# A hybrid decoder step on one Trainium2 core: another order for the 28 units of the input projection

## The chip, the cores and the metric

The kernel runs on one core of one Trainium2 chip. The metric is device time in microseconds. Three runs of the kernel before took 1135.55 to 1137.87 us, median 1137.05 us.

## The reference, cut to what matters

One layer of a decoder trunk over 512 prompt tokens and 32 sample tokens (8 sequences of 4), model width 1024, all float32:

```
x <- LN1(alpha*x + 0.5*SwiGLU_1(x))
x <- LN2(alpha*x + W_out[concat(attn_group(x), hgrn_group(x))])
x <- LN3(alpha*x + 0.5*SwiGLU_2(x))
z = x @ W_in;  columns of z: [q_att | k_att | v_att | q_hg | f_hg | i_hg | g_hg], 512 each
attn_group: 8 heads of 64, rotary q and k, dilated windows (128,1), (512,4), (2048,16),
            combined by their softmax denominators; sample tokens also read a key/value cache
hgrn_group: 4 heads of 128, f = lb + (1-lb)*sigmoid(f_hg), S_t = diag(f) S_{t-1} + (1-f) outer i_hg,
            o_t = S_t^T silu(q_hg); then per-head RMSNorm, times hg_norm_g * silu(g_hg)
```

The rotated keys and the values, the new caches and the HGRN states are outputs too.

## The kernel before, in words

Everything is kept transposed: features on the 128 partitions, the 544 tokens (16 sample, 512 prompt, 16 sample) along the free dimension, in two halves `a` of 272. A matmul of two float32 operands is done as three: each operand is split into a high part (ScalarE copies it to the rounded type, L332) and a low part (VectorE subtracts, L334), and `chunk` issues high*high, high*low and low*high (L315 to L317).

The stages are the first FFN, the mix stage (`mix`), the output projection (`project`) and the second FFN. The mix stage is built around the input projection, whose 3584 columns are cut into 28 units of 128 columns. One unit is one transfer of 512 KB (`ws`), one split, and for each half 8 chunks of 3 matmuls into a PSUM bank `ps_d` (there are two of these), which is then evacuated. A ring holds the split weights of four units (`R = 4`). The tuple `WIN` gives the order of the units. An entry is `(c, i)`: `c` is a group of 128 columns (two attention heads, or one HGRN head), called chunk here, and `i` is 0 query, 1 key, 2 value of attention, 3 forget gate, 4 query, 5 value (input), 6 output gate of HGRN. What hangs on a unit is emitted as soon as its second half is done (function `mixed` in `mix`):

- 0 and 1: evacuation to `raw` (two buffers for all queries, keys and values), rotation (`rope`: four small DMAs that swap partitions, a POOL and two VectorE operations), then stacks for the score matmuls (`q_done`, `k_done`). The low part of the keys, `klo`, has one buffer.
- 2: the values are transposed into `vn` (one buffer, `v_done`), then prompt attention of the chunk is emitted (`att_prompt`): eight steps (four query blocks, two heads) of score matmuls (L702), a masked maximum (L706), an exponential (L708), normalisation (L710), transposes (L679), a copy (L717), and value matmuls per block (L726). After chunks 1 and 3 the sample attention of two chunks follows (`att_sample`): score matmuls against the key cache (L754), value matmuls against the value cache (L784, L790).
- 5: the HGRN head is emitted (`hgrn`). Its work tiles have one buffer; the product of decays `E1` (the trace calls it E) is written by a scan at the start (L822) and last read by the state update at the end (`update`, L976).
- 6: the gate. If the unit after a value unit `(c, 5)` is `(c, 6)`, the head's end is emitted with the gate ahead of the norm; else the norm and the state update are emitted at once and the gate is multiplied in when its unit arrives:

```
if a == 1:
    part["end"] = self.hgrn(c, part)
    if WIN[j + 1] != (c, 6):
        part["end"] = part["end"]()
...
if a == 1 and i == 6:
    o[4 + c] = part["end"](part["gs"])
```

The multiplication of the gate is L964, the norm's factor is put on by L813. The results are `o[0..3]` (attention) and `o[4..7]` (HGRN).

`project` splits `o` in the order `KORD = (0, 4, 1, 5, 2, 6, 3, 7)` and contracts over these eight chunks in the same order, so a unit of the output projection can start with `o[0]` and needs `o[3]` and `o[7]` last.

The order on each engine is not the order of the program: a scheduler that plays the program through a timeline of its own while the kernel is built picks, on each engine, the earliest emitted instruction that is ready in that timeline, and hands out buffers in the same way. On the chip each engine then follows the list so made. Where a unit stands in `WIN` sets the priority of all that hangs on it.

Of the kernel before, what the change touches and what calls it, by code (L numbers as in the profile page):

```python
# [64 lines left out]
def free(t, offset, dims):  # L65
# [3 lines left out]


WIN = (
    (0, 0), (0, 4), (0, 3), (0, 5), (0, 6), (0, 1), (1, 3), (0, 2), (1, 4), (1, 0), (1, 1), (1, 5), (1, 2), (2, 3),
    (2, 0), (2, 4), (2, 1), (2, 2), (1, 6), (2, 5), (2, 6), (3, 0), (3, 1), (3, 2), (3, 4), (3, 3), (3, 5), (3, 6),
)


# [1139 lines left out]
```

## Time and profile before

| what | value |
|---|---|
| median of three runs | 1137.05 us (1135.55 to 1137.87) |
| the profiled execution | 1141.93 us, span 1140.1 us |
| mean granted TensorE clock | 0.982 |
| busy: TensorE, weight loads, VectorE, ScalarE, POOL | 96, 92, 68, 50, 33% of the span |
| mix stage: first and last evacuation of an input-projection unit | 400.3 and 655.5 us |
| first normalisation matmul of the output projection | 703.8 us |

Rows of the timeline read: start in us, duration in us, engine, line, operation, output <- inputs, shape, count, and in brackets how long the engine was idle before it and what ended that. Rows of stretches read: window, then for PE, PEld (weight loads), DVE (VectorE), ACT (ScalarE) and POOL the busy us and instruction count, then the granted clock of TensorE, the share of the DMA engines and GB/s.

### The profile page before, as it was taken

To read this page: it belongs to the slowest core of one execution; us is meant where nothing else is said; L and a number is where in the kernel's file an instruction comes from. 1 tells how busy PE (TensorE), PEld (TensorE's weight loads), DVE (VectorE), ACT (ScalarE), POOL (GpSimd) and SP (SyncE) were. 2 spreads that over 40 slices of the span, in tenths; PEclk is the share of its full clock that TensorE was granted. 3 is DMA by queue.
4 is the path that set the end of the run, shared out by engine and by line. 5 is a ranking of instruction groups with operands and counts; after the bars stand their busy time and mean duration, and the time that the engine had idled before them with its cause. 6 is when DMAs were issued, how large, how long until landed. Compare 5 with 4: busy or idle time off the path is not lost.

```text
span 1140.1 us, 21927 instructions
## 1 busy us (share of the span) xinstructions
PE 1094.2 (96%) x8666; PEld 1047.1 (92%) x8666; DVE 780.7 (68%) x1282; ACT 570.6 (50%) x1123; POOL 373.8 (33%) x420
## 2 busy tenths in 40 slices
PE   7899999999999999999999988988999999999995
PEld 7899999999999988878997858978999999999995
DVE  6868857865776965664746646788687578567766
ACT  5435533552554675566456643465355235425544
POOL 2513412430343444231411301345143125214336
PEclk9899999999999999999999978999999999999998
DMA  7344444454415385376736624504533432332122
GB/s 247 104 130 154 154 144 148 126 194 149 128 44 195 112 276 168 122 261 228 238 105 223 240 98 161 184 17 171 171 130 102 136 111 89 89 103 92 41 72 79
DMA packets 46168, 163.49 MB, mean 143 GB/s; under 512 B 6512, under 2 KB 10224, under 8 KB 45040
## 3 DMA queue, kind: packets, MB, share of 16 engines
q1 hardware_dynamic: 46064, 162.08, 43.0%
q8 instruction: 68, 1.11, 0.4%
q14 instruction: 36, 0.29, 0.1%
HBM read 150.79 MB, written 42.60 MB: 170 GB/s over the span
## 4 chain that ended last, share of the span: by engine, by line
PE 82%; DVE 7%; DMA 4%; ACT 3%; issue 2%; POOL 2%; SPq 0%; POOLq 0%; DVEq 0%; ACTq 0%
PE ps_d L278 20%; PE ps_h L278 10%; PE ps_d L316 7%; PE ps_d L315 7%; PE ps_d L317 7%; PE ps_a L278 5%; PE ps_a L316 3%; PE ps_a L315 3%; PE ps_a L317 3%; PE ps_h L317 2%; PE ps_h L315 2%; PE ps_h L316 2%; DVE wL L334 2%; PE ps_s L754 1%; PE ps_a L679 1%
## 5 line engine op out<-in xcount | busy, mean ns | idle before, releaser
L334 DVE TENSOR_TENSOR wL<-ws,wH 128x1024 fp32r<-128x1024 f32 (+3 forms) x141 | 174.2, 1236 | 80.8 <-ACT wH L332 77.7
L332 ACT ACTIVATE wH<-ws 128x1024 fp32r<-128x1024 f32 (+3 forms) x141 | 129.3, 918 | 183.4 <-PE ps_d L278 49.3
L1008 POOL TENSOR_TENSOR h<-hx,h 128x272 fp32r<-128x272 f32 x88 | 98.6, 1122 | 159.7 <-ACT h L1007 153.4
L334 DVE TENSOR_TENSOR wL<-sw,wH 128x1024 fp32r<-128x1024 f32 x78 | 117.1, 1503 | 40.2 <-ACT wH L332 40.1
L315 PE MATMUL ps_d<-xH,wH 128*128 128x272 f32 x456 | 136.2, 299 | 4.7 <-ACT xH L332 4.3
L316 PE MATMUL ps_d<-xL,wH 128*128 128x272 f32 x456 | 137.4, 301 | 3.2 <-DVE xL L405 3.0
L317 PE MATMUL ps_d<-xH,wL 128*128 128x272 f32 x456 | 135.2, 297 | 0.5 <-DVE wL L334 0.5
L332 ACT ACTIVATE wH<-sw 128x1024 fp32r<-128x1024 f32 x78 | 82.6, 1059 | 81.8 <-PE ps_d L278 29.5
L225 POOL TENSOR_TENSOR sw<-ws,sw 128x512 f32<-128x512 f32 x38 | 55.3, 1456 | 157.3 <-DVE sw L222 137.5
L315 PEld LDWEIGHTS ps_d<-xH,wH 128*128 128x128 f32 x456 | 87.4, 192 | 9.2 <-ACT xH L332 5.0
L278 PE MATMUL ps_d<-xH,wL 128*128 128x272 f32 x320 | 92.9, 290 | 1.9 <-DVE wL L334 1.9
L316 PEld LDWEIGHTS ps_d<-xL,wH 128*128 128x128 f32 x456 | 87.6, 192 | 7.5 <-DVE xL L405 3.7
L278 PE MATMUL ps_d<-tH,wH 128*128 128x272 f32 x320 | 92.9, 290 | 0.0
L278 PE MATMUL ps_d<-tH,wL 128*128 128x272 f32 x320 | 92.9, 290 | 0.0
L278 PE MATMUL ps_d<-tL,wH 128*128 128x272 f32 x320 | 92.9, 290 | 0.0
L220 POOL TENSOR_TENSOR sw<-ws 128x512 f32<-128x512 f32 x38 | 53.2, 1401 | 120.7 <-issue 48.1
L278 PE MATMUL ps_d<-xL,wH 128*128 128x272 f32 x320 | 92.4, 289 | 0.0
L278 PE MATMUL ps_d<-xH,wH 128*128 128x272 f32 x320 | 92.2, 288 | 0.0
L317 PEld LDWEIGHTS ps_d<-xH,wL 128*128 128x128 f32 x456 | 87.6, 192 | 4.1 <-issue 2.7
L315 PE MATMUL ps_d<-h,wH 128*128 128x272 f32 x240 | 69.2, 288 | 0.0
L317 PE MATMUL ps_d<-h,wL 128*128 128x272 f32 x240 | 69.0, 288 | 0.0
L316 PE MATMUL ps_d<-h,wH 128*128 128x272 f32 x240 | 68.9, 287 | 0.0
(412 smaller groups left out, 3600.8 us busy)
## 6 DMA issues: line engine op xcount, KB each, us to landing
ws<-in_w2gu SPq DMA_DIRECT2D x42, 512.0 KB, 3.9
ws<-in_w1gu SPq DMA_DIRECT2D x41, 512.0 KB, 4.5
ws<-in_win SPq DMA_DIRECT2D x28, 512.0 KB, 4.2
out_ck_out<-in_ck SPq DMA_DIRECT2D x16, 640.0 KB, 5.7
out_cv_out<-in_cv SPq DMA_DIRECT2D x16, 640.0 KB, 5.5
kv<-in_ck SPq DMA_DIRECT2D x16, 640.0 KB, 6.3
kv<-in_cv SPq DMA_DIRECT2D x16, 640.0 KB, 5.0
ws<-in_w1d SPq DMA_DIRECT2D x24, 384.0 KB, 3.2
```

The source lines that it names most:

```text
L220: g.tensor_tensor(s2[:, lo], a21, a22, op=OP.add)
L225: g.tensor_tensor(s2[:, hi], a12, s1[:, hi], op=OP.subtract)
L278: nc.tensor.matmul(ps, w[:, k, :], y, start=first and i == 0, stop=last and i == 2, skip_group_check=True)
L315: mm(o, H[:, k, :], x[0], start=first, stop=False)
L316: mm(o, H[:, k, :], x[1], start=False, stop=False)
L317: mm(o, L[:, k, :], x[0], start=False, stop=last)
L332: a = self.nc.scalar.activation(H, x, AF.Copy)
L334: v = self.nc.vector.tensor_tensor(L, x, H.bitcast(F32), op=OP.subtract)
L679: self.nc.tensor.transpose(out, x, self.ident[:n, :n])
L754: last = mm(ps[w, :384], self.qsz[:, i, s, 32 * (b + x):32 * (b + x) + 32], kc[x][:, i, 2 * s:2 * s + 3].rearrange("p s d -> p (s d)"), st ...
L1008: nc.gpsimd.tensor_tensor(L, x, H.bitcast(F32), op=OP.subtract)
```

## The change

Only the order of the units changes, from the 14th entry on. The first 13 stay. Counted from 0, chunk 1's gate (1, 6) goes from place 18 to 25 and chunk 2's gate (2, 6) from 20 to 26; chunk 3's queries, keys and values go from 21, 22, 23 to 18, 19, 21; chunk 2's HGRN value (2, 5) goes from 19 to 20; chunk 3's HGRN query, forget gate and value go from 24, 25, 26 to 22, 23, 24; chunk 2's attention query and key go from 14 and 16 to 13 and 14, its forget gate and HGRN query from 13 and 15 to 15 and 16. Since (2, 5) and (3, 5) are no longer followed by their own gates, the ends of heads 2 and 3 are emitted without the gate, which is multiplied in afterwards.

```
 WIN = (
-    (0, 0), (0, 4), (0, 3), (0, 5), (0, 6), (0, 1), (1, 3), (0, 2), (1, 4), (1, 0), (1, 1), (1, 5), (1, 2), (2, 3),
-    (2, 0), (2, 4), (2, 1), (2, 2), (1, 6), (2, 5), (2, 6), (3, 0), (3, 1), (3, 2), (3, 4), (3, 3), (3, 5), (3, 6),
+    (0, 0), (0, 4), (0, 3), (0, 5), (0, 6), (0, 1), (1, 3), (0, 2), (1, 4), (1, 0), (1, 1), (1, 5), (1, 2), (2, 0),
+    (2, 1), (2, 3), (2, 4), (2, 2), (3, 0), (3, 1), (2, 5), (3, 2), (3, 4), (3, 3), (3, 5), (1, 6), (2, 6), (3, 6),
 )
```

## The prediction, before the run

> **What bounds the kernel now.** I read the page's engine and clock rows first, then a table of stretches, then the timelines of TensorE, ScalarE, VectorE and the DMA queue through the mix stage.
>
> ```profile
> PE 1094.2 (96%) x8666; PEld 1047.1 (92%) x8666; DVE 780.7 (68%) x1282; ACT 570.6 (50%) x1123; POOL 373.8 (33%) x420
> ...
> 100.00:200.00 100.00, 100.00 (x799) 100.00 (x798) 69.03 (x92) 43.62 (x74) 30.45 (x24) 1.00 0.46 148
> ...
> 660.00:670.00 10.00, 8.34 (x64) 5.43 (x62) 3.20 (x10) 3.23 (x9) 0.00 (x0) 0.80 0.58 188
> 670.00:680.00 10.00, 9.27 (x50) 6.52 (x50) 3.88 (x14) 4.59 (x20) 0.00 (x0) 0.52 0.00 0
> 680.00:690.00 10.00, 3.88 (x29) 2.78 (x27) 6.84 (x19) 5.98 (x14) 0.00 (x0) 0.82 0.00 0
> 690.00:700.00 10.00, 10.00 (x74) 9.53 (x73) 4.82 (x14) 2.70 (x9) 0.00 (x0) 0.83 0.45 141
> ```
>
> TensorE carries the kernel: in a dense stretch it starts 799 matmuls in 100 us, 0.125 us each, so one unit of the input projection (48 matmuls) is 6.0 us. The last rows show the one hole near the change: from 660 to 690 us weight loads fall to 2.8 to 6.5 of 10 us and the granted clock to 0.52. The projection is used up there. What remains runs in two chains, and both have to end before the output projection gets its last two input chunks.
>
> ```profile
> 457.92 0.28 PE L702 MATMUL ps_a<-kst,qst 128*128 128x256 f32 x1
> 515.73 1.09 PE L726 MATMUL ps_o<-aw,vn 128*64 128x128 f32 x16
> 520.71 0.28 PE L702 MATMUL ps_a<-kst,qst 128*128 128x256 f32 x1
> 576.18 1.09 PE L726 MATMUL ps_o<-aw,vn 128*64 128x128 f32 x16
> 580.90 0.28 PE L702 MATMUL ps_a<-kst,qst 128*128 128x256 f32 x1
> 641.46 1.09 PE L726 MATMUL ps_o<-aw,vn 128*64 128x128 f32 x16
> 645.96 0.28 PE L702 MATMUL ps_a<-kst,qst 128*128 128x256 f32 x1
> 694.14 1.09 PE L726 MATMUL ps_o<-aw,vn 128*64 128x128 f32 x16
> ...
> 696.91 0.79 DVE L334 TENSOR_TENSOR xL<-z,xH 128x272 fp32r<-128x272 f32 x2 [0.94 <-ACT xH L332]
> ```
>
> These are the first score matmul and the last value matmul of prompt attention for chunks 0 to 3. Each chunk starts 3.4 to 3.9 us after the one before has ended, because klo and vn have one buffer. From 458 to 695 us attention is one unbroken chain of 57.8, 55.5, 60.6 and 48.2 us (first row to second of each pair), and the output projection's chunk 3 is ready at 697.7 us.
>
> **The change part by part.** Slots are places in the order, counted from 0.
>
> ```profile
> 556.93 0.38 ACT L524 ACTIVATE raw<-ps_d 128x272 f32<-128x272 f32 x1
> 557.71 0.40 ACT L550 ACTIVATE gs<-ps_d 128x272 f32<-128x272 f32 x1
> 563.01 0.38 ACT L550 ACTIVATE gs<-ps_d 128x272 f32<-128x272 f32 x1
> ...
> 570.81 0.37 ACT L539 ACTIVATE iT<-ps_d 128x272 f32<-128x272 f32 x1
> ...
> 581.44 0.38 ACT L550 ACTIVATE gs<-ps_d 128x272 f32<-128x272 f32 x1
> ...
> 598.51 0.38 ACT L524 ACTIVATE raw<-ps_d 128x272 f32<-128x272 f32 x1
> ...
> 611.33 0.38 ACT L524 ACTIVATE raw<-ps_d 128x272 f32<-128x272 f32 x1
> ```
>
> (a) No unit is added or removed: 28 times 6.0 us, 28 weight transfers, the same evacuations, ropes and splits. Sum 0. It is a move, and the rows give the clock time of each slot (slot 17 ends at 556.9, slot 18 at 563.0, 19 at 570.8, 20 at 581.4, 22 at 598.5, 23 at 611.3).
>
> (b) Chunk 2's values stay at slot 17 (556.9), 20 us ahead of the end of attention 1 that gates them; chunk 3's values move from slot 23 to 21 but attention 3 waits for attention 2 (642.5), not for them. So neither attention chain starts earlier: 0.
>
> (c) Chunk 3's queries and keys move from slots 21 and 22 to 18 and 19, three slots (27.7 us by 598.5 less 570.8, some 20 once the 6.8 us of waiting below are taken off). With them go eight rope DMAs, a K output, and the rope and stack work on POOL, VectorE and ScalarE. Sample attention of the second head pair needs exactly these keys:
>
> ```profile
> 605.72 1.50 PE L754 MATMUL ps_s<-kv,qsz 128*32 128x384 f32 x16
> ...
> 663.74 0.35 DVE L710 TENSOR_SCALAR aw<-aw,stat 128x256 f32<-128x256 f32 x1
> 665.20 1.20 PE L784 MATMUL ps_s<-kv,pz 128*32 128x256 f32 x16 [1.54 <-DMA kv<-in_cv]
> 668.01 0.61 PE L679 MATMUL ps_h<-mats,smp 128*32 128x128 f32 x2
> 668.79 0.69 PE L679 MATMUL ps_a<-mats,aw 128*128 128x128 f32 x2
> ```
>
> Its scores begin at 605.7 now and can begin some 20 us earlier; its last value matmuls then lie near 645, under the projection, not at 665. Now they wait for a cache transfer with TensorE empty for 1.54 us, and attention 3's transposes, whose input was ready at 664.09, stand behind them until 668.79: 4.7 us. That wait ends. Bounds: nothing gained (dense matmuls stand there instead) and 4.7. The step it sits in took 7.45 us (661.68 to 669.13); the three before it, with TensorE full, took 15.72, or 5.24 each. I take the difference, -2.2.
>
> ```profile
> 661.68 0.36 PE L702 MATMUL ps_a<-kst,qst 128*128 128x256 f32 x1
> ...
> 669.13 0.67 PE L702 MATMUL ps_a<-kst,qst 128*128 128x384 f32 x1
> ...
> 675.36 0.42 DVE L710 TENSOR_SCALAR aw<-aw,stat 128x384 f32<-128x384 f32 x1
> 675.73 0.82 PE L315 MATMUL ps_d<-xH,wH 128*128 128x272 f32 x2
> 679.04 0.80 PE L679 MATMUL ps_a<-mats,aw 128*128 128x128 f32 x3
> 681.45 1.28 ACT L435 ACT_TABLE_LOAD   x1
> 683.50 0.72 ACT L708 ACTIVATE aw<-aw,stat 128x512 f32<-128x512 f32 x1
> ```
>
> (d) Gates 1 and 2 go from slots 18 and 20 to 25 and 26: 12.0 us of dense work into the tail. On the chain it costs nothing as long as it fills the hole of (660, 690); if it stands in front of attention's own matmuls it costs up to 12. It keeps TensorE busy, so the rows above at a clock of 0.52 run faster: the output-projection matmuls ahead of the transposes hold them from 675.78 to 679.04 (3.3 us); at full clock that is 3.3 x 0.52 = 1.7, so I take -1.5 (bounds 0 and -3.3). Four evacuations (0.8 us ScalarE each) and their VectorE steps also move there; both engines are under 7 of 10 us busy, and if one lands ahead of an exponential it costs 0.8. I take +0.5 (bounds 0 and 3.2). The table load ahead of the exponential at 683.50 stays: 0 (bounds -2.0 and 0).
>
> (e) Queues. The rope DMAs go ahead of later weight transfers on SP's queue and wait there for raw. The weight ring holds four units, 24 us of dense work, which covers that; with the cover gone the longest such wait is 7.1 us:
>
> ```profile
> SPq L627 <- ACT raw L524: 10.0, 3, 7.1
> ```
>
> Sum: -2.2 - 1.5 + 0.5 = -3.2 us. The profiled execution took 1141.93 us, 4.9 above the median of the runs, so it would be 1138.7, and the median 1137.05 would be 1133.9. The terms' ends give -10.0 to +3.2; the 12 us of (d) standing in front of attention are a rival below.
>
> **The rivals.** First, slower: the HGRN chain. HGRN 3 cannot write E until HGRN 2's state update has read it.
>
> ```profile
> 569.14 0.69 DVE L676 TENSOR_TENSOR klo<-raw,kst 64x512 fp32r<-64x512 f32 x1
> ...
> 630.03 1.12 DVE L976 SCALAR_TENSOR_TENSOR st<-st,E,ps_h 128x128 f32<-128x128 f32 x4
> 637.62 1.29 DVE L822 TENSOR_TENSOR_SCAN E<-mats,sf 128x544 f32<-128x544 f32 x1
> ...
> 679.97 0.73 DVE L964 SCALAR_TENSOR_TENSOR z<-z,gs 128x544 f32<-128x544 f32 x1 [4.19 <-ACT z L945]
> ...
> 690.32 0.43 DVE L334 TENSOR_TENSOR xL<-z,xH 128x272 fp32r<-128x272 f32 x1
> ```
>
> HGRN 2's values move from slot 19 to 20, from 570.8 to 581.4. Its update ends 60.3 us after them, so at 641.8. There is a second delay: slot 18 now needs a raw buffer, and of the two one holds chunk 2's values and the other its keys until 569.83. The first half, ready at 557.7, is stuck for 12.1 us; TensorE fills the other ps_d bank by 563 and then has none for up to 6.8 us, so HGRN 2 may end at 648.6. HGRN 3's scan follows (I allow 1 us) at 642.8 to 649.6, where it was 637.62. From scan to split input took 53.1 us; with the gate now after the norm (0.73, the L964 row) chunk 7 is ready at 696.7 to 703.5. It is needed at 699.2 (697.7, and 12 matmuls of chunk 3 ahead of it). So this chain decides from an end of HGRN 2 at 644.3 on, and at its late end it costs 4.3: 1141.4 us. Against it: its transposes at 668.01 stood behind the same cache wait and matmuls, 668.01 less 665.20 plus 1.54, 4.35 us that it gets back if (c) holds; then it decides only from 648.7 on.
>
> On that stuck evacuation the Trainium skill ("PSUM — Partial Sum Buffer", section "Engine vs sequencer instructions") says that ScalarE's queue is strictly first-in first-out, which speaks against the change: attention's exponentials queued behind it would wait too. By that rule the sum would be worse by up to those 12.1 us, if the order put them there; no run here shows it at this place, and the other sentences go without it.
>
> Second, no change: the dense work of the gates stands where the sample matmuls stood, and attention 3 keeps its 48.2 us. For it speaks (b): nothing makes the chain start earlier. 1137 us.
>
> Third, slower by filling: with TensorE full attention 3 takes the mean of chunks 0 to 2, 58.0 us: +9.8, 1146.9. Against it: the total work is the same, and only 12 us are moved.
>
> Fourth, a larger gain through the clock. Busy time from 660 to 700 times what the clock lacked is 8.34 x 0.20 + 9.27 x 0.48 + 3.88 x 0.18 + 10.0 x 0.17 = 8.5 us. If the fillers hold the clock at 1.00 and all of it lies on the chain, 1128.5 us. The Trainium skill ("TensorE: Matmul & The Clock Gate", section "What's actually happening") says that the array falls to half clock after an idle window of about 3.4 us and recovers after one of activity; the 0.52 agrees. Against it: the long holes of 3 us wait on VectorE, and remain.
>
> **How the numbers follow.** The forecast (gain of 2.4 to 7 us, own range 1130.0 to 1134.7) has 0.35 and the clock case 0.10: faster 0.45. No change has 0.27. The HGRN chain has 0.22 and filling 0.06: slower 0.28. Within 0.2% (2.3 us) is what a measurement here cannot tell from no change. Leaving out the outer parts of the clock and filling cases, the range is 1126 to 1145.
>
> **What would show it.** Right: sample attention's last value matmuls (L784) before 655; the clock above 0.8 between 660 and 690; the last L726 some 3 us earlier than 694.1. Wrong: HGRN 3's scan (L822) after 646 and chunk 7's split after chunk 3's; an L524 evacuation waiting near 560 to 570 with TensorE idle; or attention 3 taking more than 50 us.

## The result: 0.9% slower

The changed kernel takes 1146.38 us (median of four runs, 1146.26 to 1149.76) against 1136.30 us: a ratio of 1.0091, 95% interval [1.0071, 1.0111]. Forecast were 1133.9 us and a range of 1126 to 1145; the time lies above both. The profiled execution of the changed kernel took 1149.76 us (span 1147.9), 3.4 above its median, that of the kernel before 1141.93, 5.6 above the new median. From the first normalisation copy behind the mix stage (line L351) to the end of the span both need the same time (1147.9 - 711.3 = 436.6 and 1140.1 - 702.5 = 437.6 us). The first evacuation of an input-projection unit, at 400.5 and 400.3 us, is not late either. So the whole loss arises in the mix stage. What is late in the profile of the changed kernel is so by up to 3.4 us more than in its median run. Because the first profile of before lies high, a second one is set beside it below (before2, 1135.71 us, span 1133.8).

The engines' row of the page after: TensorE starts as many matmuls as before and is busy 3.9 us longer; the other engines do the same work, but for one ScalarE instruction fewer.

```profile
PE 1098.1 (96%) x8666; PEld 1050.6 (92%) x8666; DVE 779.2 (68%) x1282; ACT 567.9 (49%) x1122; POOL 374.0 (33%) x420
```

Stretches of 10 us of the changed kernel, columns as before the prediction (window; PE, PEld, DVE, ACT and POOL busy; granted clock; DMA share; GB/s):

```profile
520.00:530.00 10.00, 7.75 (x67) 6.38 (x65) 5.40 (x14) 7.06 (x19) 3.60 (x12) 1.00 0.18 40
...
570.00:580.00 10.00, 8.01 (x44) 7.58 (x44) 3.49 (x7) 3.44 (x8) 2.94 (x6) 0.66 0.24 76
...
680.00:690.00 10.00, 7.53 (x61) 5.03 (x60) 4.60 (x15) 6.45 (x21) 0.00 (x0) 0.86 0.45 146
690.00:700.00 10.00, 9.03 (x61) 8.08 (x59) 1.38 (x4) 5.00 (x14) 0.00 (x0) 0.80 0.01 2
700.00:710.00 10.00, 7.29 (x33) 6.38 (x32) 7.69 (x21) 0.75 (x2) 0.00 (x0) 0.71 0.33 107
```

The reader is to see two new holes in the middle of the projection (67 and 44 matmuls, where the kernel before starts 96 and 97 by its second profile) and that the tail's hole is not filled but has moved from 660 to 690 to 680 to 710. The timeline of the changed kernel shows what the holes wait for and what becomes late (bracket: idle time ahead of the instruction and what ended it):

```profile
523.99 0.40 PE L315 MATMUL ps_d<-xH,wH 128*128 128x272 f32 x1 [2.25 <-ACT raw L524]
560.43 0.38 ACT L524 ACTIVATE raw<-ps_d 128x272 f32<-128x272 f32 x1
569.48 0.63 PE L679 MATMUL ps_a<-mats,aw 128*128 128x128 f32 x4 [1.86 <-DVE aw L710]
571.34 0.69 DVE L676 TENSOR_TENSOR klo<-raw,kst 64x512 fp32r<-64x512 f32 x1
572.11 0.69 ACT L524 ACTIVATE raw<-ps_d 128x272 f32<-128x272 f32 x2
572.56 0.59 PE L315 MATMUL ps_d<-xH,wH 128*128 128x272 f32 x1 [1.99 <-ACT raw L524]
581.44 1.09 PE L726 MATMUL ps_o<-aw,vn 128*64 128x128 f32 x16
585.30 0.40 ACT L524 ACTIVATE raw<-ps_d 128x272 f32<-128x272 f32 x1
592.51 0.38 ACT L539 ACTIVATE iT<-ps_d 128x272 f32<-128x272 f32 x1
642.73 0.28 PE L702 MATMUL ps_a<-kst,qst 128*128 128x256 f32 x1
653.25 0.34 SPq L978 DMA_DIRECT2D out_ss<-st  x1
654.84 1.28 DVE L822 TENSOR_TENSOR_SCAN E<-mats,sf 128x544 f32<-128x544 f32 x1
660.90 1.07 PE L784 MATMUL ps_s<-kv,pz 128*32 128x256 f32 x16
694.85 1.09 PE L726 MATMUL ps_o<-aw,vn 128*64 128x128 f32 x16
703.20 0.71 DVE L964 SCALAR_TENSOR_TENSOR z<-z,gs 128x544 f32<-128x544 f32 x1
705.51 0.78 DVE L334 TENSOR_TENSOR xL<-z,xH 128x272 fp32r<-128x272 f32 x2
707.62 0.34 SPq L978 DMA_DIRECT2D out_ss<-st  x1
711.32 0.43 ACT L351 ACTIVATE zr<-z 128x272 fp32r<-128x272 f32 x1 [6.62 <-DMA out_ss<-st]
```

Both TensorE holes wait for an evacuation into `raw`. Chunk 3's queries (both halves at 572.11) needed a `raw` buffer, which came free when `klo` of chunk 2 had been made (571.34, ends 572.03). Head 2's values, at 570.8 before, come at 592.51; the write of its state (653.25) and head 3's scan (654.84, before 637.6) are late in turn. Head 3 then ends the stage: its gate (behind the norm now) at 703.20, chunk 7's split at 705.51, state write issued at 707.62, and only when that write has landed does the first copy of the next stage start, 711.32. Attention 3 began 3 us earlier than before and took 52 us. The same events in the second profile of the kernel before:

```profile
570.47 0.37 ACT L539 ACTIVATE iT<-ps_d 128x272 f32<-128x272 f32 x1
575.84 1.09 PE L726 MATMUL ps_o<-aw,vn 128*64 128x128 f32 x16
637.27 1.29 DVE L822 TENSOR_TENSOR_SCAN E<-mats,sf 128x544 f32<-128x544 f32 x1
645.61 0.28 PE L702 MATMUL ps_a<-kst,qst 128*128 128x256 f32 x1
685.27 0.43 DVE L334 TENSOR_TENSOR xL<-z,xH 128x272 fp32r<-128x272 f32 x1
689.72 1.09 PE L726 MATMUL ps_o<-aw,vn 128*64 128x128 f32 x16
692.49 0.79 DVE L334 TENSOR_TENSOR xL<-z,xH 128x272 fp32r<-128x272 f32 x2 [0.94 <-ACT xH L332]
694.71 0.34 SPq L978 DMA_DIRECT2D out_ss<-st  x1
697.83 0.43 ACT L351 ACTIVATE zr<-z 128x272 fp32r<-128x272 f32 x1 [5.05 <-issue]
```

Here chunk 7's split ends at 685.7, ahead of attention's end and of chunk 3's split (692.49). In the changed kernel chunk 3's split starts at 699.48 and chunk 7's, last of all, at 705.51.

### The profile page after: what moved, and what is told of

Its sections match the earlier page's. It is cut to its first block, busy times and chain, and to the rows that moved or that the text cites. A ratio compares the mean times of both kernels' runs of the same rounds, so it can differ in the third digit from the quotient of the medians.

```text
span 1147.9 us, 21933 instructions
## 1 busy us (share of the span) xinstructions
PE 1098.1 (96%) x8666; PEld 1050.6 (92%) x8666; DVE 779.2 (68%) x1282; ACT 567.9 (49%) x1122; POOL 374.0 (33%) x420
## 4 chain that ended last, share of the span: by engine, by line
PE 79%; DVE 9%; ACT 4%; DMA 3%; issue 3%; POOL 1%; SPq 0%; POOLq 0%; DVEq 0%; ACTq 0%
PE ps_d L278 19%; PE ps_h L278 10%; PE ps_d L315 7%; PE ps_d L316 7%; PE ps_d L317 7%; PE ps_a L278 5%; PE ps_a L316 3%; PE ps_a L315 3%; PE ps_a L317 3%; PE ps_h L315 2%; PE ps_h L317 2%; PE ps_h L316 2%; DVE wL L334 2%; PE ps_s L754 1%; PE ps_a L679 1%
## 5 line engine op out<-in xcount | busy, mean ns | idle before, releaser
L332 ACT ACTIVATE wH<-ws 128x1024 fp32r<-128x1024 f32 (+3 forms) x141 | 129.3, 918 | 184.0 <-PE ps_d L278 47.3
L315 PE MATMUL ps_d<-xH,wH 128*128 128x272 f32 x456 | 139.5, 306 | 10.4 <-ACT xH L332 5.9
L317 PE MATMUL ps_d<-xH,wL 128*128 128x272 f32 x456 | 136.9, 301 | 0.5 <-DVE wL L334 0.5
L332 ACT ACTIVATE wH<-sw 128x1024 fp32r<-128x1024 f32 x78 | 82.6, 1059 | 82.5 <-PE ps_d L278 29.3
L225 POOL TENSOR_TENSOR sw<-ws,sw 128x512 f32<-128x512 f32 x38 | 55.3, 1455 | 156.6 <-DVE sw L222 118.1
L315 PEld LDWEIGHTS ps_d<-xH,wH 128*128 128x128 f32 x456 | 89.5, 196 | 16.6 <-ACT xH L332 6.9
L278 PE MATMUL ps_d<-xH,wH 128*128 128x272 f32 x320 | 92.2, 288 | 0.0
L317 PEld LDWEIGHTS ps_d<-xH,wL 128*128 128x128 f32 x456 | 89.5, 196 | 2.4 <-issue 1.2
L315 PE MATMUL ps_d<-h,wH 128*128 128x272 f32 x240 | 69.3, 289 | 0.0
L317 PE MATMUL ps_d<-h,wL 128*128 128x272 f32 x240 | 69.2, 288 | 0.0
```

The source lines that it names most:

```text
L225: g.tensor_tensor(s2[:, hi], a12, s1[:, hi], op=OP.subtract)
L278: nc.tensor.matmul(ps, w[:, k, :], y, start=first and i == 0, stop=last and i == 2, skip_group_check=True)
L315: mm(o, H[:, k, :], x[0], start=first, stop=False)
L317: mm(o, L[:, k, :], x[0], start=False, stop=last)
L332: a = self.nc.scalar.activation(H, x, AF.Copy)
```

## The experiments

Four explanations stood against each other. **The chain (U):** head 2's late values make head 3 late, and head 3 ends the stage. **The end:** only the last piece counts (chunk 7's split, the state update), and could be cut there. **Stalls (R):** TensorE's idle and slow time in the middle is the loss itself, wherever the chains stand. **Filling (F):** the gates moved into the tail stand in front of attention 3. Ratios are to the kernel before on the same chip. The expectations use more letters: H is the chain with chunk 7 as its end, T the end with head 3's state write as its last piece, A attention 3 as the end.

### Is it the end of head 3?

a_no7 gives the output projection chunk 6 where it needs chunk 7. a_no7_noupd also leaves out head 3's state update. a_upd and b_upd emit that update ahead of head 3's norm, in the changed kernel and in the one before.

```
a_no7:        self.split(..., o[min(k, 6)][:, a, :])
a_no7_noupd:  the same, and  if h < 3: update()   (head 3's state is written as loaded)
a_upd, b_upd: if h == 3: update()   # ahead of the norm, instead of after it
```

> Leaves out one wait: the output projection reads chunk 6 again in place of chunk 7 (HGRN head 3), all else of the changed kernel stays. Theory H (HGRN head 3 ends last, its split was 6 us behind that of attention chunk 3, 706.3 against 700.3): 6 us less than the changed kernel, 1139 to 1142. Theory R (the loss is TensorE time lost while evacuations wait for a raw buffer near 522 and 570): unchanged, 1145 to 1148. Theory F (the gate units moved to the end stand in front of attention 3): unchanged, 1145 to 1148.

> The changed kernel; the output projection reads chunk 6 in place of chunk 7, and the state update of HGRN head 3 is left out (its state goes out as it came, right after its load). So neither result of head 3 is waited for at the end. Theory T: the stage ends with attention 3, whose split is near 700: 1136 to 1140. Theory R (the loss is TensorE time lost while evacuations wait for raw): 1144 to 1147. Theory F (gate units stand in front of attention 3): 1144 to 1147.

> The changed kernel with the state update of HGRN head 3 emitted ahead of its norm and not held behind it. Theory T: its write lands before 700, what is left of head 3 is chunk 7 (split near 706), so 3 us less: 1142 to 1144.5. Theories R and F: unchanged, 1145 to 1148.

> The same edit in the kernel before. Theory T: there too the state write landed last (702.4, against 699.5 for the first output-projection unit), so 2 to 3 us less: 1133 to 1135. Theory A: unchanged within 1 us of 1136.4.

Measured: a_no7 1146.87 us, 1.0092 [1.0064, 1.0120]; a_no7_noupd 1142.18, 1.0065 [1.0045, 1.0084]; a_upd 1146.83, 1.0102 [1.0084, 1.0120]; b_upd 1135.35, 1.0002 [0.9989, 1.0015]. H and T missed in all four (1139 to 1142 for a_no7, 1136 to 1140 for a_no7_noupd, 1142 to 1144.5 for a_upd, 1133 to 1135 for b_upd); a_no7 and a_upd came out where R and F had them, a_no7_noupd between. Without chunk 7 nothing is gained, because the next stage then still waits for the state write. The timeline of a_no7:

```profile
708.75 0.34 SPq L978 DMA_DIRECT2D out_ss<-st  x1
711.84 0.75 ACT L351 ACTIVATE zr<-z 128x272 fp32r<-128x272 f32 x2 [3.66 <-DMA out_ss<-st]
```

The update alone being earlier gains nothing either by the medians, since chunk 7 is still late (its profile has L351 5.0 us earlier, at 706.31, but the changed kernel's profile is itself 3.4 above its median). In the kernel before, the first copy also comes 3.1 us behind the issue of the write (before2: 697.83 and 694.71), but b_upd gains nothing, so the write is not what the time hangs on there. With both off the end the time falls by 3 of the 10 us by the ratios (4.2 by the medians, which come from two chips; the intervals overlap, so this size is rough), and the last split is then attention's chunk 3, at 697.70, where before2 has it at 692.02. So head 3's end costs some 3 to 4 us and both its pieces must go; the rest stays, with attention's end 5.7 us late.

### Is it the buffers?

Two edits to the changed kernel, each with room made in memory by smaller `ksa`, `vnew` and `rec`: a second buffer for E, and a third for raw.

```
a_E2:   E1, dd = T("E1", 2), T("E2")
a_raw3: part[name] = tile("raw", 3)
```

> The changed kernel with two buffers for E1, so that HGRN head 3 need not wait for the state update of head 2 (room for it from a smaller new-value and new-key tile; the order of instructions of the changed kernel does not change by that room). Theory H: the scan of head 3 starts some 12 us earlier (bounded then by the second scan's tile, free near 642), chunk 7 is ready near 694 instead of 706, attention 3 ends last: 1138 to 1142. Theory R: the stalls near 522 and 570 are untouched, 1145 to 1148. Theory F: 1145 to 1148.

> The changed kernel with three raw buffers. Theory H: HGRN head 2's values are evacuated near 582 instead of 592, so head 3 starts and ends some 10 us earlier, attention 3 ends last: 1138 to 1142. Theory R: the whole loss goes, the two TensorE stalls and the low clock at 570 to 580 with it: 1135 to 1139. Theory F: unchanged, 1145 to 1148.

Measured: a_E2 1152.07 us, 1.0136 [1.0107, 1.0166]; a_raw3 1146.16, 1.0079 [1.0052, 1.0107]. Neither brings the time back, and H missed in both (1138 to 1142). In a_E2 head 3's scan comes at 638.91 instead of 654.84, but its later step L877 at 664.30, no better than the 665.21 of the changed kernel: the head's other tiles also have one buffer, which would explain that freeing E moves the scan alone. But the run is not the changed kernel with E freed and all else equal: TensorE waits 3.62 us for POOL at 483 (0.96 in the changed kernel), and head 2's values come at 598.56, 6.0 us later. Its TensorE lost 21.0 us from 400 to 585, that of the changed kernel 16.0 (the measure is explained at the table below). That is about as much as it is slower, 5.7 us by the medians; the cause of the new wait stays open. In a_raw3 the wait moves by one unit, from the queries to the keys:

```profile
576.67 0.69 DVE L676 TENSOR_TENSOR klo<-raw,kst 64x512 fp32r<-64x512 f32 x1
578.05 0.67 ACT L524 ACTIVATE raw<-ps_d 128x272 f32<-128x272 f32 x2
578.48 0.39 PE L315 MATMUL ps_d<-xH,wH 128*128 128x272 f32 x1 [2.57 <-ACT raw L524]
590.90 0.38 ACT L539 ACTIVATE iT<-ps_d 128x272 f32<-128x272 f32 x1
```

A third buffer lets the queries through, and the keys, which also stand ahead of (2, 5), wait in their place. Head 2's values come 1.6 us earlier than in the changed kernel, head 3's scan 6.0 (648.83), and the median stays. So the run doesn't tell the chain from R: the values are still late, and TensorE still loses 10.2 us from 515 to 585.

### Which part of the order?

before2 is the kernel before again, for its profile. Then the change was taken apart: places 13 to 16 (chunk 2's units), places 18 to 20 ((2, 5) behind or ahead of (3, 0) and (3, 1)), and the gates at the end.

```
after:     (2,0)(2,1)(2,3)(2,4)(2,2) (3,0)(3,1)(2,5)      (3,2)(3,4)(3,3)(3,5)(1,6)(2,6)(3,6)
a_25:      (2,0)(2,1)(2,3)(2,4)(2,2) (2,5)(3,0)(3,1)      (3,2)(3,4)(3,3)(3,5)(1,6)(2,6)(3,6)
a_c2order: (2,3)(2,0)(2,4)(2,1)(2,2) (3,0)(3,1)(2,5)      (3,2)(3,4)(3,3)(3,5)(1,6)(2,6)(3,6)
b_gates:   (2,3)(2,0)(2,4)(2,1)(2,2) (2,5)(3,0)(3,1)      (3,2)(3,4)(3,3)(3,5)(1,6)(2,6)(3,6)
b_qkv:     (2,3)(2,0)(2,4)(2,1)(2,2) (3,0)(3,1)(1,6)(2,5)(2,6)  (3,2)(3,4)(3,3)(3,5)(3,6)
late25:    (2,3)(2,0)(2,4)(2,1)(2,2) (1,6)(3,0)(2,5)(3,1) (3,2)(3,4)(3,3)(3,5)(2,6)(3,6)
```

> The kernel before once more, for a second profiled execution: the first took 1141.93 us where the median is 1136.4. Theory T (the mix stage ends when the state write of HGRN head 3 has landed, which lets the next stage's memory pool open): the first normalisation copy (L351) follows that landing, near 698 to 702 us, and what follows it to the end takes 436 to 438 us as in every profile so far. Theory A (attention 3 sets the end): L351 follows the first output-projection unit instead, with the state write landed earlier.

> The changed kernel with chunk 2's HGRN value unit (2, 5) ahead of chunk 3's query and key. Theory H: head 2's values come near 566 to 572, as before the change, head 3's scan near 637, attention 3 ends last: 1136 to 1141. Theory R: chunk 3's query then comes a slot later, when a raw buffer is free, so the stall near 570 goes and that near 522 stays: 1139 to 1143. Theory F: 1145 to 1148.

> The changed kernel with chunk 2's queries, keys, forget gate and HGRN query back in the order of before (slots 13 to 16). It takes away the first of the two stalls, near 522, alone. Theory U: the second stall and the place of (2, 5) stay, so little changes: 1143.5 to 1147. Theory R (every us of TensorE lost to a raw wait is paid): 2 to 3 us less than the changed kernel, 1143 to 1144.5. Theory F: 1145 to 1148.

> The kernel before with only the two gates moved to the end; chunk 2's HGRN value unit (2, 5) so comes to slot 18, chunk 3's queries, keys and values to 19 to 21. Theory U (the loss comes from the order of (2, 5) and chunk 3's queries and keys: HGRN head 2 starts 22 us late, head 3 waits for it and piles up with attention 3; the gates at the end cost little): no stall near 522 or 570, head 2's values near 566: 1134 to 1139. Theory F (dense work at the end stands in front of attention 3, whatever comes before): 1143 to 1148.

> The kernel before with only chunk 3's queries and keys moved, from slots 21 and 22 to 18 and 19; the gates stay in the middle, so (2, 5) comes at slot 21. Theory U: its values are evacuated near 600 (slot 21 and the wait for a raw buffer), head 2 ends near 660, head 3 begins after it, 25 us later than before: 1147 to 1156, worse than the whole change. Theory F: no dense work is moved to the end, 1134 to 1139.

> The kernel before with slots 18 to 27 of the order made (1,6),(3,0),(2,5),(3,1),(3,2),(3,4),(3,3),(3,5),(2,6),(3,6): head 2's values are projected one slot later than before (slot 20, as in the changed kernel), but only one unit, chunk 3's queries, stands ahead of them and not two. Theory 'the chain': head 2's values come one unit of some 10 us later than before's 570.8, at 578 to 583, its update ends near 641 and head 3's scan stands at 642 to 646 (before 637.6, after 654.8); the time is 1137.5 to 1141. Rival 'stalls of TensorE': only the waits for a raw buffer cost; with one unit ahead they are about half of the changed kernel's, and the time is 1140 to 1142 if they are there and 1134 to 1136.5 if they are not, wherever head 3's scan stands.

The times of the profiles are starts in us; the splits are those of the output projection (L332). The last column is TensorE time lost from 515 to 585, summed over stretches of 1 us: the time it was not busy, and of its busy time the share that the granted clock lacked. It is one execution each; the changed kernel's order gave 8.8 to 11.6 in a_no7_noupd, a_upd and a_no7.

| kernel | time, us | ratio to before | head 2's values | head 3's scan | chunk 7's split | chunk 3's split | L351 | TensorE lost, us |
|---|---|---|---|---|---|---|---|---|
| before2 | 1135.71 | (one run) | 570.5 | 637.3 | 684.8 | 692.0 | 697.8 | 0.6 |
| b_gates | 1134.10 | 0.9978 [0.9966, 0.9991] | 562.4 | 626.5 | 681.8 | 689.9 | 692.9 | 0.3 |
| late25 | 1137.36 | 1.0007 [0.9995, 1.0019] | 580.8 | 642.8 | 689.4 | 686.2 | 697.9 | 1.4 |
| a_25 | 1138.96 | 1.0023 [1.0010, 1.0037] | 565.5 | 628.0 | 683.0 | 694.5 | 699.6 | 2.6 |
| b_qkv | 1142.93 | 1.0051 [1.0032, 1.0071] | 598.0 | 660.5 | 700.3 | 696.2 | 709.5 | 7.6 |
| a_c2order | 1143.16 | 1.0063 [1.0039, 1.0088] | 589.7 | 651.1 | 696.3 | 691.2 | 703.7 | 7.0 |
| after | 1146.38 | 1.0091 [1.0071, 1.0111] | 592.5 | 654.8 | 704.0 | 698.9 | 711.3 | 9.7 |

The first four rows of the list of orders are a square: two parts, each with and without the other. The gates alone (b_gates; the units behind them move up a place or two) make the kernel 0.22% faster. From there (2, 5) behind chunk 3's queries and keys adds 0.85 of a per cent (a_c2order), chunk 2's order 0.45 (a_25), and both together 1.13, 12.8 us of 1136. By the timelines each part hits one of the two chains.

*(2, 5) hits the HGRN chain.* Timeline of a_c2order:

```profile
566.42 0.60 PE L315 MATMUL ps_d<-xH,wH 128*128 128x272 f32 x1 [1.99 <-ACT raw L524]
574.99 1.09 PE L726 MATMUL ps_o<-aw,vn 128*64 128x128 f32 x16
589.72 0.37 ACT L539 ACTIVATE iT<-ps_d 128x272 f32<-128x272 f32 x1
651.05 1.28 DVE L822 TENSOR_TENSOR_SCAN E<-mats,sf 128x544 f32<-128x544 f32 x1
703.71 0.43 ACT L351 ACTIVATE zr<-z 128x272 fp32r<-128x272 f32 x1 [6.68 <-DMA out_ss<-st]
```

Attention is no later than before's here (attention 1 ends 574.99, chunk 3's split stands at 691.2), yet the stage ends late, and on the state write: head 3 sets it. From head 2's values to head 3's scan it is 61 to 67 us in every row of the table, so the scan moves with the values.

*Chunk 2's order hits the attention chain.* Timeline of a_25:

```profile
523.27 0.39 PE L315 MATMUL ps_d<-xH,wH 128*128 128x272 f32 x1 [2.28 <-ACT raw L524]
565.52 0.38 ACT L539 ACTIVATE iT<-ps_d 128x272 f32<-128x272 f32 x1
582.42 1.09 PE L726 MATMUL ps_o<-aw,vn 128*64 128x128 f32 x16
628.03 1.28 DVE L822 TENSOR_TENSOR_SCAN E<-mats,sf 128x544 f32<-128x544 f32 x1
699.62 0.43 ACT L351 ACTIVATE zr<-z 128x272 fp32r<-128x272 f32 x1 [4.41 <-DVE z L580]
```

Head 3 is early (628.03), but with the keys straight behind the queries TensorE waits for raw at 523, attention 1 ends at 582.42 (b_gates 576.95), and chunk 3's split is last, at 694.5 (689.9).

b_qkv, the move of queries and keys without the rest, is slower as the chain has it, but by less than expected (1147 to 1156, worse than the whole change). Its scan is the latest of all and its L351 nearly so, with 431.8 us from there to the end where the other rows have 435 to 438. Only 39.7 us pass from its scan to chunk 7's split, where the changed kernel takes 49.1 and b_gates 55.3. So lateness of the scan is not passed on one for one; that it depends on what else TensorE has to do then is likely, but not shown.

late25 was to tell lateness from stall. One unit ahead of (2, 5) also brings a raw wait (both halves of the queries at 570.21), but TensorE keeps a clock of 1.00 there and loses only 1.4 us.

```profile
570.21 0.66 ACT L524 ACTIVATE raw<-ps_d 128x272 f32<-128x272 f32 x2
580.82 0.38 ACT L539 ACTIVATE iT<-ps_d 128x272 f32<-128x272 f32 x1
642.84 1.29 DVE L822 TENSOR_TENSOR_SCAN E<-mats,sf 128x544 f32<-128x544 f32 x1
692.84 0.34 SPq L978 DMA_DIRECT2D out_ss<-st  x1
697.93 0.43 ACT L351 ACTIVATE zr<-z 128x272 fp32r<-128x272 f32 x1 [7.76 <-DVE z L580]
```

The scan stands where the chain put it (642 to 646), and the time, just below the chain's 1137.5 to 1141, can't be told from before's: head 2 ten us late is still covered. The rival's two values (1140 to 1142 with the waits, 1134 to 1136.5 without) both miss 1137.36, but they took the waits for half of the changed kernel's. With the 1.4 us that were lost, R would be right too: that is 0.8 us more than before2 loses, and the ratio makes the kernel 0.8 us slower.

So R is not refuted. By the ratios the kernels differ from before by -2.5 (b_gates), 0.8 (late25), 2.6 (a_25), 5.8 (b_qkv), 7.2 (a_c2order) and 10.3 us (after), and the last column, counted from before2, follows that to within 2.2 us, b_qkv included, which the scan's start does not. R had a_c2order right (1143 to 1144.5), which the chain missed by 0.3 us, and missed a_25, which the chain had right, by less than 0.1. For the chains speak a_c2order, where attention is not late and the next stage waits for head 3's write, the 3 to 4 us of a_no7_noupd, and the square: counted from b_gates, the lost TensorE time leaves 2.8 to 3.4 us of each of the other three corners unexplained. No run makes head 2 twenty us late without stalling TensorE, or stalls it as long with head 2 in time, so the shares of the two are not separated. Common to both is the wait for a raw buffer.

F falls with b_gates, which puts the same gates into the tail and is faster than both kernels, and with b_qkv, which leaves them in the middle and is slower. In b_gates the first copy of the next stage is

```profile
692.85 0.43 ACT L351 ACTIVATE zr<-z 128x272 fp32r<-128x272 f32 x1 [2.18 <-DVE z L580]
```

5.0 us ahead of before2's.

## Why the prediction was wrong

**(a) No work added, sum 0:** right for the work, 8666 matmuls in both. But the sum has no term for what the order does to TensorE: the wait for raw stands only in a rival, and from 515 to 585 TensorE lost 9.7 us by waits and a lower clock, where before2 loses 0.6.

**(b) "Neither attention chain starts earlier: 0":** the step failed, for it allowed only for an earlier start. Places 13 to 16 were costed at nothing, and they lengthen attention 1: it ends at 581.44, not 576.18. a_25 against b_gates prices that part at 0.45%, some 5 us.

**(c) Sample attention leaves the tail, -2.2:** its scores do begin about 19 us earlier (586.57), and the last value matmuls no longer wait for the cache. But they run until 662 beside head 3, not until 645: 4.3 us earlier than the profile before, 3.4 than before2. Units that start earlier did not end earlier by as much.

**(d) Gates into the tail, -1.0 with its +0.5:** not visible in the changed kernel, since the hole had moved. Alone the gates bring -0.22% [-0.34, -0.09], -2.5 us, near the -3.2 forecast for everything. How much of it is the clock was not separated: in b_gates attention 3 also begins 3.7 us earlier than in before2, and the sample scores begin at 586.76, as (c) wanted it.

**(e) Queues:** held in size. The wait of SP's queue for raw grew from 7.1 to 10.4 us at most, and no weight transfer is what TensorE waits for in the holes.

**The first rival named what the traces show, a wait for raw and a late head 2, and was under-sized.** It said: head 2 late, head 3's scan late, decisive from an end of HGRN 2 at 644.3 on. late25 agrees with that point: its head 2 ends at 642.8, with no measurable cost. The failed term is the start of head 2's values. Forecast were 581.4 and up to 6.8 of stall, 588.2; measured 592.5. Slot by slot against the rows of before, 3.5 us come from chunk 2's order (slot 17 at 560.43 for 556.93), 5.6 from the raw stall (slot 18 at 572.11 for 563.01, less the 3.5), 5.4 from the keys' slot (585.30 for 570.81, less 9.1), run in part at a clock of 0.50, and 3.4 are won back at (2, 5), 7.2 us instead of 10.6. Head 2 takes 60.7 us, forecast 60.3. So the scan came at 654.84, past the forecast 642.8 to 649.6. Nor did the price stop at 4.3. In the profile of the changed kernel that is because the end was taken to be chunk 7's split, while the next stage also waits for the state write behind it, and the 4.35 us set against the rival as relief from the sample matmuls did not come. What TensorE's lost time adds beside this stays open, as said above.

Beside the forecast stood the Trainium skill's "PSUM — Partial Sum Buffer", section "Engine vs sequencer instructions", by which ScalarE's queue is strictly in order, so that exponentials behind the stuck evacuation would wait up to 12.1 us. The trace doesn't go against it, but the case did not arise: the exponential of attention 1 (571.34) stands ahead of the stuck evacuation (572.11) in the list.

**The third rival (filling)** had the sign of one effect, attention 3 at 52 us instead of 48.2 and 44.1. But it is not the gates: its first three steps, over by 667, take 24.3 us against before2's 15.9, while head 3 and the sample matmuls share TensorE. That its price, 1146.9, lies next to the measured time is luck. The wrong-signs named ahead of the run all appeared: a scan after 646, chunk 7's split after chunk 3's, an L524 wait with TensorE idle, attention 3 over 50 us.

**The clock rival** did not come about: 0.86, 0.80 and 0.71 from 680 to 710, only later than before's 0.80, 0.52 and 0.82. So the sign that was to show a gain, a clock above 0.8 from 660 to 690, did appear (1.00, 1.00, 0.86), and there was no gain.

The weighing failed, more than the listing: the raw stall was found in the profile before and then given 0.22, against -3.2 us of small terms each read off one execution, itself 5.6 us from the median. The range's ends, 1126 and 1145, are not worked out from any term.

## What to carry to other kernels

Before a unit is moved earlier, list what it pushes later and follow that to the end of the stage: here the moved queries and keys could not use their earlier place (their buffer came free with attention 1), while the unit that they pushed back headed a serial chain of 60 us. Where two chains end a stage, price both, with the slack between them: here ten us of lateness went without a measurable loss, and twenty with one of 7 to 10, TensorE's stalls included. Price those stalls too, for TensorE was busy 96% of the span. Take a reordering apart into its moves: one of the three was a gain, and alone it beats both kernels (1134.10 us).

## What the runs showed of the hardware

The granted clock fell after short waits. TensorE was idle for 1.86 and 1.99 us shortly before 573 (569.48 and 572.56 above). Stretches of the changed kernel around them:

```profile
568.00:570.00 2.00, 0.52 (x5) 0.55 (x6) 1.30 (x3) 0.00 (x0) 2.00 (x4) 1.00 0.73 272
570.00:571.00 1.00, 0.57 (x3) 0.14 (x2) 0.39 (x1) 0.60 (x1) 0.69 (x2) 1.00 0.65 262
571.00:572.00 1.00, 0.00 (x0) 0.00 (x0) 0.97 (x3) 0.66 (x2) 0.00 (x0) 0.54 0.54 217
574.00:575.00 1.00, 1.00 (x7) 1.00 (x6) 0.00 (x0) 0.00 (x0) 0.00 (x0) 0.50 0.59 137
```

The clock goes from 1.00 to 0.50 and stays there until just before 578; the 0.66 of the stretch from 570 to 580 is a mean of the two. At 0.50 the L315 to L317 matmuls start 0.227 us apart, at 1.00 some 0.125. The Trainium skill ("TensorE: Matmul & The Clock Gate", section "What's actually happening") puts the fall at an idle window of some 3.4 us and the level at half. The level agrees with the 0.50 here. The longest unbroken wait was 1.99 us, and TensorE was busy 1.09 of the 4 us from 568 to 572, so the fall did not need one unbroken wait of 3.4 us.

A stage's first instruction can wait for the landing of the last stage's write: 3.7 us from issue (707.62) to the first copy (711.32), 3.1 in a_no7. That the next stage takes over the last one's memory is how the kernel's pools are laid out. And two executions of the same kernel put their tail's slow stretch at different places (0.52 in 670 to 680, 0.51 in 680 to 690) and differ by 6.2 us (1141.93 and 1135.71), about twice the effect that was forecast.
